# A softmax on one core: the first store enters the transfer queue when group 4 has been scaled

## The chip, the core and the metric

The kernel runs on one core of a Trainium2 chip. A core has engines that work side by side, each with its own list of instructions: VectorE (DVE), ScalarE (ACT) and GpSimd (POOL) compute, SyncE (SP) here only waits and issues transfers. TensorE (PE) has no work in this kernel. Data move between the large memory (HBM) and the core's own memory (SBUF, 128 partitions) by transfers (DMAs) that run on 16 transfer engines of the core. The metric is the device time of one execution in microseconds (us).

## What is computed

A softmax over the last axis of an input of 16 x 1024 x 512 numbers of 4 bytes, that is 16,384 rows of 512, 33.55 MB in and 33.55 MB out:

```
x_max = np.max(x, axis=-1, keepdims=True)
exp_x = np.exp(x - x_max)
return exp_x / np.sum(exp_x, axis=-1, keepdims=True)
```

## The kernel before

**Tiles.** The 16,384 rows are taken as 128 rows per partition: each of the 128 partitions has 128 rows, numbered 0 to 127. Eight such rows on all partitions make a group (`GROUP`, 128x4096 numbers); there are 16 groups. Transfers move blocks of 16 rows per partition (`BLOCKS`), so two groups, 4096 KB each. There are eight loads and eight stores. I number both 0 to 7: load 0 and store 0 are the block (0, 16), load 5 is (80, 96), and so on. Within a block, a partition's 16 rows lie together in HBM, so one packet is 32 KB.

**The buffer.** `held` has room for 96 rows per partition (`RING`, 12 groups). Six blocks fit. Loads 6 and 7 reuse the place of blocks 0 and 1, and so must wait until stores 0 and 1 have landed.

**What is done to a group.** DVE takes the negated maximum of each row (`rowmax`, line 164). ACT takes the exponential of each row in place, with that maximum as bias, and sums it (line 195, eight instructions for a group). DVE takes the reciprocal of the sums (line 170), and the group is multiplied by it (line 172): by POOL for groups 0 to 11, by DVE for groups 12 to 15. The order of DVE's work is written out by hand in `VECTOR` (M is a maximum, P a scaling on POOL, V one on DVE).

**The order of transfers.** All 16 transfers are issued by SP into one queue, in the order of `ORDER`: loads 0 to 5, stores 0 to 2, loads 6 and 7, stores 3 to 7. The first six loads wait for nothing (`AHEAD`), and the first of them is moved ahead of the program's opening barrier (`loads_at_the_head`). Behind them, the loop of lines 140 to 154 writes SP's list. For a load it puts a wait for the store that must have landed (`stored`) ahead of the issue. For a store it puts waits for the groups that the block holds: each group `g` has a semaphore `scaled[g]`, which the scaling of that group raises, and the set `done` sees to it that each is waited for once:

```
for g in range(GROUPS):
    if meets(k, *group(g)) and g not in done:
        take(nc.sync, scaled[g], 1)
        done.add(g)
```

So store 0 waits for groups 0 and 1, store 1 for groups 2 and 3, store 2 for groups 4 and 5. `take` (line 110) is a wait on the engine's own list: what stands behind it on that engine waits too. After the last issue SP waits for all stores to land, which ends the program.

Of the kernel before, what the change touches and what calls it, by code (L numbers as in the profile page):

```python
# [1 line left out]

# [4 lines left out]

F32 = mybir.dt.float32
EXP = mybir.ActivationFunctionType.Exp
AX = mybir.AxisListType.X  # L10

GROUP = 8
GROUPS = 16
RING = 12 * GROUP

BLOCKS = [(0, 16), (16, 32), (32, 48), (48, 64), (64, 80), (80, 96), (96, 112), (112, 128)]
ORDER = [
    ("L", (0, 16)),
    ("L", (16, 32)),
    ("L", (32, 48)),
    ("L", (48, 64)),
    ("L", (64, 80)),
    ("L", (80, 96)),
    ("S", (0, 16)),
    ("S", (16, 32)),  # L30
    ("S", (32, 48)),
    ("L", (96, 112)),
    ("L", (112, 128)),
    ("S", (48, 64)),
    ("S", (64, 80)),
    ("S", (80, 96)),
    ("S", (96, 112)),
    ("S", (112, 128)),
]
AHEAD = 6  # L40

VECTOR = """
    M0 M1 P0 M2 P1 M3 P2 M4 P3 M5 P4 M6 P5 M7 P6 M8 P7 M9 P8 M10 P9 M11
    P10 M12 P11 M13 V12 M14 V13 M15 V14 V15
"""

AT_HEAD = {mybir.EngineType.SP: 1}

def loads_at_the_head(nc):

    main, body = nc.main_func.blocks[0], nc.main_func.blocks[1]
    for engine, count in AT_HEAD.items():
        loads = [
            i
            for i in body.instructions
            if i.engine == engine and type(i).__name__ == "InstDMACopy"  # L60
        ][:count]
        barrier = next(
            n
            for n, i in enumerate(main.instructions)
            if i.engine == engine and type(i).__name__ == "InstDrain"
        )
        for load in loads:
            body.instructions.remove(load)
        main.instructions[barrier:barrier] = loads


@with_exitstack
def kernel(
    ctx: ExitStack,
    tc: tile.TileContext,
    x: bass.AP,
    out: bass.AP,
):
    nc = tc.nc
    nc.at_finalize(loads_at_the_head)  # L80
    P = nc.NUM_PARTITIONS

    d = x.shape[-1]
    x_rows, out_rows = x.flatten_outer_dims(), out.flatten_outer_dims()
    assert x_rows.shape[0] == GROUPS * GROUP * P

    def in_dram(rows, a, b):

        first, last = next(k for k in BLOCKS if k[0] <= a and b <= k[1])
        block = rows[first * P : last * P].rearrange("(p r) d -> p r d", p=P)  # L90
        return block[:, a - first : b - first, :]

    held = nc.alloc_sbuf_tensor("held", [P, RING, d], F32).ap()
    shift = nc.alloc_sbuf_tensor("shift", [P, GROUPS * GROUP], F32).ap()
    sums = nc.alloc_sbuf_tensor("sums", [P, GROUPS * GROUP], F32).ap()
    recip = nc.alloc_sbuf_tensor("recip", [P, GROUPS * GROUP], F32).ap()

    loads = [k for what, k in ORDER if what == "L"]
    stores = [k for what, k in ORDER if what == "S"]
    loaded = {k: nc.alloc_semaphore(f"loaded{k[0]}") for k in loads}  # L100
    scaled = [nc.alloc_semaphore(f"scaled{g}") for g in range(GROUPS)]
    stored = {k: nc.alloc_semaphore(f"stored{k[0]}") for k in stores}
    maxed = nc.alloc_semaphore("maxed")
    expd = nc.alloc_semaphore("expd")
    to_pool = nc.alloc_semaphore("to_pool")
    to_vector = nc.alloc_semaphore("to_vector")

    def take(engine, semaphore, n):

        engine.wait_ge(semaphore, n).then_inc(semaphore, -n)  # L110

    def rows(a, b):
        assert a // RING == (b - 1) // RING
        return held[:, a % RING : (b - 1) % RING + 1, :]

    def meets(k, a, b):
        return k[0] < b and a < k[1]

    def group(g):
        return g * GROUP, (g + 1) * GROUP  # L120

    def stats(t, g):
        return t[:, g * GROUP : (g + 1) * GROUP]

    def load(k):
        copy = nc.sync.dma_start(out=rows(*k), in_=in_dram(x_rows, *k))
        copy.then_inc(loaded[k], 16)
        return copy

    with tc.manual_schedule():
        for _, k in ORDER[:AHEAD]:
            tc.no_tile_sem_insts.add(load(k).ins.name)
    tc.close()
    tc.compile()  # L137

    taken, done = set(), set()
    for what, k in ORDER[AHEAD:]:  # L140
        if what == "L":
            for s in stores:
                if meets(s, k[0] - RING, k[1] - RING) and s not in taken:
                    take(nc.sync, stored[s], 16)
                    taken.add(s)
            load(k)
        else:
            for g in range(GROUPS):
                if meets(k, *group(g)) and g not in done:
                    take(nc.sync, scaled[g], 1)  # L150
                    done.add(g)
            nc.sync.dma_start(out=in_dram(out_rows, *k), in_=rows(*k)).then_inc(
                stored[k], 16
            )


    seen = set()

    def rowmax(g):
        for k in loads:  # L160
            if meets(k, *group(g)) and k not in seen:
                take(nc.vector, loaded[k], 16)
                seen.add(k)
        nc.vector.reduce_max(  # L164
            out=stats(shift, g), in_=rows(*group(g)), axis=AX, negate=True
        ).then_inc(maxed, 1)

    def scale(g, engine, ready):
        take(nc.vector, expd, 1)
        nc.vector.reciprocal(out=stats(recip, g), in_=stats(sums, g)).then_inc(ready, 1)  # L170
        take(engine, ready, 1)
        engine.tensor_mul(  # L172
            out=rows(*group(g)),
            in0=rows(*group(g)),
            in1=stats(recip, g).unsqueeze(2).to_broadcast([P, GROUP, d]),
        ).then_inc(scaled[g], 1)

    for step in VECTOR.split():
        what, g = step[0], int(step[1:])
        if what == "M":  # L180
            rowmax(g)
        elif what == "V":
            scale(g, nc.vector, to_vector)
        else:
            scale(g, nc.gpsimd, to_pool)


    nc.scalar.preload_act_table(EXP)  # L188

    with nc.scalar.Fori(0, GROUPS) as i:  # L190
        take(nc.scalar, maxed, 1)
        for r in range(GROUP):
            row = held[:, bass.ds(i % (RING // GROUP) * GROUP + r, 1), :]
            at = bass.ds(i * GROUP + r, 1)
            act = nc.scalar.activation(  # L195
                out=row,
                in_=row,
                func=EXP,
                bias=shift[:, at],
                scale=1.0,  # L200
                accum_out=sums[:, at],
            )
        act.then_inc(expd, 1)


    for k in stores:
        if k not in taken:
            take(nc.sync, stored[k], 16)


# [1 line left out]
_INS = ['x']  # L212
_OUTS = [((16, 1024, 512), 'float32')]


# [23 lines left out]
```

## Time and profile before

| | before |
|---|---|
| time, median of 3 runs | 160.15 us (160.12 to 160.21) |
| the profiled execution | 160.14 us, its span 158.8 us |
| busy: DVE, ACT, POOL | 90.6 (57%), 92.0 (58%), 84.0 us (53%) |
| one scaling on POOL (line 172) | 7015 ns, x12 |
| one scaling on DVE (line 172) | 4570 ns, x4 |
| one row maximum on DVE (line 164) | 4399 ns, x16 |
| one exponential on ACT (line 195) | 712 ns, x128 |
| loads, issue to landing | 12.2 / 29.7 / 58.8 us (shortest, median, longest) |
| stores, issue to landing | 17.9 / 28.3 / 38.3 us |

The span is the stretch from the first to the last instruction of the program; the rest of the execution's time lies around it. A time within the span is counted from its start. "Issue to landing" is the time from SP's issue of a transfer to the moment when its semaphore shows that all of it has arrived, so it holds the time that the transfer stands in the queue behind others. In the view by stretches, each line is a stretch of the span, its length, and what happened in it: the share in which the 16 transfer engines were busy, and the GB/s that they moved. A packet is counted whole in the stretch in which it starts, which is why the share of a short stretch can be over 1.

### The profile page before, as it was taken

The numbers are of one execution on the slowest core, as the hardware profiler recorded it, in microseconds if no ns is written. First come the engines' busy times: TensorE is split into PE (matmuls) and PEld (weight loads), VectorE is DVE, ScalarE is ACT, GpSimd is POOL, SyncE is SP. The second block draws the span as 40 slices with busy tenths as digits, with TensorE's granted clock in tenths as the row PEclk, the third lists the DMA queues.
The fourth block names the chain that finished last, engine by engine and source line by source line (L and its number), as shares of the span: only waits on it lengthen the run. The fifth ranks groups of instructions, "written<-read, shape, count | busy, mean of one in ns | idle before, by whom it ended". The sixth has DMA issues, their size and how long they took to land. (4 is left out here: it accounts for less than half of the span.)

```text
span 158.8 us, 747 instructions
## 1 busy us (share of the span) xinstructions
DVE 90.6 (57%) x36; ACT 92.0 (58%) x257; POOL 84.0 (53%) x16
## 2 busy tenths in 40 slices
DVE  0008959777977977887700000795999998640000
ACT  0300699999999999999993000059934929200000
POOL 0000009999999999999999999259200000000000
DMA  7999999999999998999999999999999999999996
GB/s 264 470 454 396 413 487 421 396 454 470 396 396 487 437 396 380 413 396 454 470 396 421 462 437 396 446 479 396 421 446 454 396 437 473 413 404 454 446 413 264
DMA packets 2305, 67.12 MB, mean 423 GB/s; under 512 B 256, under 2 KB 256, under 8 KB 256
## 3 DMA queue, kind: packets, MB, share of 16 engines
q1 hardware_dynamic: 2304, 67.11, 98.9%
q14 instruction: 1, 0.01, 0.0%
HBM read 33.55 MB, written 33.55 MB: 423 GB/s over the span
## 5 line engine op out<-in xcount | busy, mean ns | idle before, releaser
L195 ACT ACTIVATE held<-held,shift x128 | 90.3, 712 | 40.0 <-ACTq L110 40.0
L172 POOL TENSOR_TENSOR held<-held,recip 128x4096 f32<-128x4096 f32 x12 | 83.8, 7015 | 28.0 <-POOLq L110 28.0
L164 DVE TENSOR_REDUCE shift<-held 128x8 f32<-128x4096 f32 x16 | 70.3, 4399 | 33.2 <-DVEq L110 33.2
L195 ACT ACTIVATION_READ_ACCUMULATOR held<-held,shift x128 | 24.6, 192 | 0.0
L172 DVE TENSOR_TENSOR held<-held,recip 128x4096 f32<-128x4096 f32 x4 | 18.3, 4570 | 0.6
L170 DVE RECIPROCAL recip<-sums 128x8 f32<-128x8 f32 x16 | 3.2, 201 | 16.5 <-DVEq L110 16.5
L188 ACT ACT_TABLE_LOAD x1 | 1.3, 1283 | 3.9 <-PEq L137 3.9
L223 POOL MEMSET const-float32-0.0<- 128x1 f32 x1 | 0.1, 98 | 0.2 <-issue 0.2
L223 POOL MEMSET const-uint8-127<- 128x1 uint8 x1 | 0.1, 102 | 0.0
L223 POOL MEMSET const-bfloat16-1.0<- 128x1 bf16 x1 | 0.1, 101 | 0.0
L223 POOL MEMSET const-float32-1.0<- 128x1 f32 x1 | 0.1, 98 | 0.0
## 6 DMA issues: line engine op xcount, KB each, us to landing
held<-in_x_dram SPq DMA_DIRECT2D x8, 4096.0 KB, 29.7
out_dram<-held SPq DMA_DIRECT2D x8, 4096.0 KB, 28.3
```

The source lines that it names most:

```text
L164: nc.vector.reduce_max(out=stats(shift, g), in_=rows(*group(g)), axis=AX, negate=True).then_inc(maxed, 1)
L170: nc.vector.reciprocal(out=stats(recip, g), in_=stats(sums, g)).then_inc(ready, 1)
L172: engine.tensor_mul(out=rows(*group(g)), in0=rows(*group(g)), in1=stats(recip, g).unsqueeze(2).to_broadcast([P, GROUP, d]),).then_inc(scal ...
L188: nc.scalar.preload_act_table(EXP)
L195: act = nc.scalar.activation(out=row, in_=row, func=EXP, bias=shift[:, at], scale=1.0, accum_out=sums[:, at],)
L223: nc = _bacc.Bacc("TRN2", target_bir_lowering=False, num_devices=1)
```

## The change

A table `AFTER` names, for a block that is stored, one more group that must have been scaled before its store is issued. It has one entry: the store of block (0, 16) also waits for group 4. The loop that writes SP's waits looks the table up:

```diff
+AFTER = {(0, 16): 4}
...
             for g in range(GROUPS):
-                if meets(k, *group(g)) and g not in done:
+                if (meets(k, *group(g)) or AFTER.get(k) == g) and g not in done:
                     take(nc.sync, scaled[g], 1)
                     done.add(g)
```

With it store 0 waits for groups 0, 1 and 4, store 1 for groups 2 and 3, and store 2 for group 5 alone, since group 4 has been waited for by then. The order in which the transfers are issued is the same, and so are the lists of DVE, ACT and POOL.

## The prediction

> **What bounds the kernel now.** I read the queue table of the page first, because the share of the transfer engines decides whether anything else matters; then the timeline of SP and POOL, which dates the issue that is moved; then the landings of single transfers; then stretches of 1.21 us, cut to one packet per engine, to see where the stream loses time.
>
> From the page, the queue and the volume (queue, packets, MB, share of 16 engines):
>
> ```profile
> q1 hardware_dynamic: 2304, 67.11, 98.9%
> HBM read 33.55 MB, written 33.55 MB: 423 GB/s over the span
> ```
>
> One queue holds everything, 16 transfers of 4096 KB, and it is busy for 98.9% of the span. So the time is the length of this stream, and the change can only matter by a hole that it closes or opens in it. The stretches below show what a full stream is. Columns: stretch in us, its length, clock, share of the transfer engines, GB/s; a packet counts where it starts.
>
> ```profile
> 0.00:1.00 1.00, 1.00 0.00 0
> 1.00:1.50 0.50, 1.00 3.12 852
> 1.50:2.00 0.50, 1.00 0.53 197
> 2.00:2.75 0.75, 1.00 0.00 0
> 2.75:3.40 0.65, 1.00 1.90 807
> ...
> 54.88:56.09 1.21, 1.00 1.01 433
> 56.09:57.30 1.21, 1.00 1.01 433
> 57.30:58.51 1.21, 1.00 1.14 433
> 58.51:59.72 1.21, 1.00 1.59 433
> 59.72:60.93 1.21, 1.00 0.44 190
> 60.93:62.14 1.21, 1.00 1.01 433
> ...
> 59.72:60.60 0.88, 1.00 0.00 0
> 60.60:61.20 0.60, 1.00 2.04 874
> 61.20:61.80 0.60, 1.00 0.00 0
> 61.80:62.40 0.60, 1.00 2.02 874
> ...
> 107.82:109.03 1.21, 1.00 1.01 433
> 109.03:110.24 1.21, 1.00 1.01 433
> ```
>
> A stretch of 1.21 us with 433 GB/s is 524 KB: one packet of 32 KB on each of 16 engines, a round. A transfer is 8 rounds, about 9.7 us. One stretch breaks the rhythm: 59.72 to 60.93 us has 190 GB/s, so 1.21 x (1 - 190/433) = 0.68 us is missing, and the two stretches ahead of it already have a share of 1.14 and 1.59: their packets take longer. This is the place where load 5 (the sixth, rows 80 to 96) ends and store 0 begins. The landings agree. Load 4 is issued at 2.16 us and lands 48.9 later, at 51.1; load 5 is issued at 2.65 and lands here:
>
> ```profile
> L126 SPq DMA_DIRECT2D held<-in_x_dram x1: 487/487/487, 2.6 to 2.6; - x1
> DMA to landing us min/median/max: 58.8/58.8/58.8
> ```
>
> That is 61.4, so 10.4 us after load 4 in place of 9.7: 0.7 us lost. By the first packets it is a little more: store 0 starts at 60.6, and eight rounds of 1.21 after load 5's first packets (about 50.1) would be 59.8. I call it the pause, 0.7 to 0.87 us, 0.8 in the sum. The other change from loading to storing (load 7 to store 3, near 109.1) has two full stretches and no pause; nor has store 2 to load 6.
>
> Now the issues and what they wait for:
>
> ```profile
> 0.00 3.13 SPq L126 DMA_DIRECT2D held<-in_x_dram  x6
> 37.54 28.23 SPq L152 DMA_DIRECT2D out_dram<-held  x3
> ...
> 51.36 7.01 POOL L172 TENSOR_TENSOR held<-held,recip 128x4096 f32<-128x4096 f32 x1
> ```
>
> Store 0 goes out at 37.54, when the queue still holds more than 20 us of loads. Group 4 is the fifth scaling of POOL, 51.36 + 7.01 = 58.37 us.
>
> **The change, part by part.** No instruction of DVE, ACT or POOL is added, removed or moved. On SP the wait for group 4 moves from store 2 to store 0.
>
> - *The wait.* SP gets past it at 58.40 and issues store 0 at 58.40 + 0.07 = 58.47 (before, the same step took 37.47 to 37.54). That is 20.9 us later.
> - *What is queued behind it on SP.* Store 1 went out at 51.49 and now follows store 0, with two waits of 0.07 that are met and an issue of 0.35: about 58.96. Its data are due 9.7 us after store 0's, so this costs nothing. Store 2 still waits for group 5 (65.37) and goes out at 65.44 as before. Load 6 waits for store 0 to land (71.2) while two more stores, 19.4 us, are queued, so its delay by any fraction of a microsecond is covered. At the end the last store is issued at 140.91 and can start only when store 6 is through, which lands at 125.56 + 23.5 = 149.1: some 7 us of cover. POOL and DVE wait for none of these issues.
> - *Does the queue run dry?* Load 5's data, without the pause, end at 59.8 on the first engines and about 60.3 on the last (the rounds are spread over 0.5 us). What an issue into idle engines costs is shown once, by load 0: issued at 0.00, 13 of 16 first packets start between 1.0 and 1.5 us, three between 1.5 and 2.0, and the second round starts between 2.75 and 3.40. So a first round takes 1.7 to 1.9 us where a warm one takes 1.21. Put behind 58.47: store 0's first packets at 59.5 to 60.4, its second round at 61.2 to 61.9. Before, the second round started from 61.8 to 62.4. If load 0 is the right pattern and nothing is added, the stream is ahead by 0.5 to 0.6: I take 0.55.
> - *Bounds.* Below: the pause goes and the store is there in time, second round at 59.8 + 1.21 = 61.0: ahead by 0.8. Above: the cold first round of load 0 and the pause on top, 61.55 + 0.87 = 62.4 on average against 62.1, behind by 0.3; if these engines take as long to start again as load 0's slowest (up to 0.4 later than its average), behind by 0.5 or a little more.
> - *Sum.* The profiled execution took 160.14 us, its span 158.8, so 1.3 lie around the span; the median of the runs shown is 160.15. 160.14 - 0.55 = 159.6.
>
> The Trainium skill speaks against the change: "DMA: Bandwidth & Descriptors", section "Rules for kernel authors", says to issue a transfer early and wait for it late, so that its fixed setup cost lies beside other work. By that rule issuing 20.9 us later can only expose a cost; it is the rival with the dry queue below. In this trace store 0 was issued early, and the pause is there all the same. The same page, "Two DMAs through the same engine are not ordered", states that transfers on one queue start in order but are pipelined, with the reading and the writing side of an engine separate; that would let a queued store begin inside load 5's last packets, and the shares of 1.14 and 1.59 before the missing stretch agree with it.
>
> **The rivals.**
>
> - *The pause belongs to the first store wherever it comes* (the first transfer out of the buffer or into the output): for it, that no later change of direction has it. Then it is paid between 59.5 and 60.4 as it was between 58.5 and 60.6, and the time stays at 160.1. Against: load 0 was the first of everything too, and its first round cost only 0.5 to 0.7 beyond a warm one.
> - *The pause goes whole.* The store that lies queued for 20 us slows the last loads, and one that arrives with their end doesn't; the engines take it over warm. 160.14 - 0.8 = 159.3. Against: store 3 lies queued for 28 us (issued at 81.5, running from 109) and slows nothing.
> - *The queue runs dry* (slower). Group 4 is ready 1.4 us before load 5's data end, and load 0 shows 1.0 to 1.9 from issue to first packet. The engines go idle, start cold, and the first store's own pause comes after it, uncovered: 0.3 to 0.6 behind, 160.5 with a reach to 160.7. It decides from the point where store 0's second round starts later than 62.1 on average, 3.6 us after its issue in place of load 0's 3.1.
> - *It doesn't do what it says.* SP's order shows store 0 behind groups 0, 1 and 4, store 1 behind 2 and 3, store 2 behind 5. If group 4 were ready no later than now that is 58.4 in any case. I give it nothing of its own.
>
> **How the numbers follow.** What a measurement of this kernel can tell from no change is about 0.2%, 0.32 us: below 159.83 is faster, above 160.47 slower. Forecast (ahead by 0.35 to 0.7, 159.6): 0.34. Pause gone whole (159.3): 0.16. Same pause, same place (160.1): 0.18. Dry queue (160.5 to 160.7 and a little beyond): 0.32, high because the cover is shorter than the slowest start that load 0 shows. So faster 0.50, same 0.18, slower 0.32. The range reaches from the pause gone whole, 159.25, to the dry queue's 160.65; the forecast's own is 159.4 to 159.8.
>
> **What would show it.** Right: load 5 lands near 60.7 in place of 61.4; the stretches of 1.21 us up to 59.7 keep a share of 1.0; store 0, issued at 58.5, has its first packets between 59.5 and 60.4, some of them 1.7 to 2.1 us long, and lands near 70.6; every later landing is earlier by the same 0.5, and the last store's issue keeps its cover. Wrong: load 5 still lands at 61.4 (the pause isn't the queued store's doing); or no packet starts for more than 1.5 us around 60 (dry). A span shorter than 158.8 with all landings up to store 0 unchanged would mean that the gain is not from here.

## The result and the profile after

The changed kernel takes 160.64 us (median of 14 runs, 160.49 to 161.36) against 160.13 us for the kernel before (14 runs beside it): ratio 1.0037, 95% interval 1.0027 to 1.0048. It is slower by 0.5 us. I had forecast 159.6.

The profiled execution took 161.36 us with a span of 160.0, more than the median. A second trace of the same kernel, the first of the experiments below, has 160.54 and 159.2. Both lose time at the same places; in the first, one engine loses about 1 us more than the others.

The queue and the volume of the kernel after (queue, packets, MB, share of 16 engines):

```profile
q1 hardware_dynamic: 2304, 67.11, 98.5%
HBM read 33.55 MB, written 33.55 MB: 419 GB/s over the span
```

The same bytes in the same number of packets, 4 GB/s slower. SP's issues in the timeline of the kernel after (start, length, count):

```profile
0.00 3.18 SPq L129 DMA_DIRECT2D held<-in_x_dram  x6
58.45 7.30 SPq L155 DMA_DIRECT2D out_dram<-held  x3
70.51 10.14 SPq L129 DMA_DIRECT2D held<-in_x_dram  x2
80.84 60.43 SPq L155 DMA_DIRECT2D out_dram<-held  x5
```

Store 0 goes out at 58.45, as worked out. Now the stream of the kernel after in stretches of one round, at the three places where the direction changes: load 5 to store 0, store 2 to load 6, load 7 to store 3 (columns as in the prediction):

```profile
56.23:57.44 1.21, 1.00 1.01 433
57.44:58.65 1.21, 1.00 1.01 433
58.65:59.86 1.21, 1.00 1.01 433
59.86:61.07 1.21, 1.00 1.01 433
...
86.41:87.62 1.21, 1.00 1.00 433
87.62:88.83 1.21, 1.00 1.28 433
88.83:90.04 1.21, 1.00 0.96 406
...
105.01:106.22 1.21, 1.00 1.00 433
106.22:107.43 1.21, 1.00 1.38 433
107.43:108.64 1.21, 1.00 1.41 406
108.64:109.85 1.21, 1.00 0.44 190
109.85:111.06 1.21, 1.00 1.01 433
```

The pause at 60 us is gone without a trace: every stretch is full, and store 0 follows load 5 without a gap. But around 88 us packets grow longer (share 1.28), and at 106 to 110 us stands the pattern that was at 57 to 61 before: two stretches with a raised share (here 1.38 and 1.41), then one with 190 GB/s. In the kernel before, the same two places are full:

```profile
88.46:89.67 1.21, 1.00 0.94 406
89.67:90.88 1.21, 1.00 1.01 433
...
107.81:109.02 1.21, 1.00 1.01 433
109.02:110.23 1.21, 1.00 1.01 433
```

(The 406 is one packet that starts a little outside its stretch; the next is on time.)

To compare runs I use one number for each place. The 16 engines report the landing of a transfer one by one; I take the mean of the 16 times, subtract that of the transfer ahead, and subtract the 9.69 us that 16 rows take at full rate (fewer for a transfer that was cut). What is left is lost. Store 2 and load 6 are added up, since the change from storing to loading shifts a landing from the one to the other.

| kernel | store 0 issued | load 5 | store 2 + load 6 | load 7 | sum |
|---|---|---|---|---|---|
| before | 37.5 us | 0.76 | 0.02 | 0.03 | 0.81 |
| after, first trace | 58.5 us | 0.03 | 0.29 | 0.98 | 1.30 |
| after, second trace | 58.6 us | 0.03 | 0.32 | 0.85 | 1.20 |

The sum rises by 0.4 to 0.5, and the median by 0.51. So at its own place the change won 0.73 us, more than was forecast. It lost 0.3 and 0.8 to 0.95 us at two places 30 and 50 us later, which had been free.

### The profile page after: what moved, and what is told of

Same layout as the page of the kernel before. It is cut to its first block, busy times and chain, and to the rows that moved or that the text cites. A ratio compares the mean times of both kernels' runs of the same rounds, so it can differ in the third digit from the quotient of the medians.

```text
span 160.0 us, 747 instructions
## 1 busy us (share of the span) xinstructions
DVE 90.6 (57%) x36; ACT 92.0 (57%) x257; POOL 84.0 (52%) x16
```

## The experiments

**The two kernels again, and other groups for store 0.** The first question was whether the places are fixed, or chance.

> The changed kernel, unaltered, for a second trace. Theory 'moved toll' (a load that ends with a store already lying in the queue pays a pause once; store 0 issued late only passes it on to the next such place): load 5 lands near 60.7 us with full stretches, as in the first trace, and a loss of about 1 us stands again at the end of load 7 (106 to 110 us) and perhaps a third of a us at the end of store 2 (87 to 89.5). Theory 'chance' (other traffic on the chip stops the stream now and then): the losses stand elsewhere, or are missing. Theory 'dry queue': a hole in the stream around 60 us and none later. The single packet of 2.7 us on one engine in the first trace should not be back, so the span should be near 159.3.

> The kernel before, unaltered, for a second trace. Moved toll: the pause of 0.7 to 0.9 us stands again at the end of load 5 (58.5 to 60.6 us), and the ends of store 2 and load 7 are full; span 158.8. Chance: the pause stands elsewhere or is missing.

```diff
-AFTER = {(0, 16): 4}
+AFTER = {(0, 16): 3}
```

> Store 0 waits for group 3 in place of group 4, so it is issued near 51.5 us, 7 us before the place where load 5 slows down. Moved toll: this is queued early enough, the pause of 0.7 to 0.9 us is back at the end of load 5, the end of load 7 is full again, and the time is that of the kernel before, 160.1. If any lateness of store 0 costs by itself, the time lies between 160.1 and 160.6, with the loss at load 7.

The same line with a 5:

> Store 0 waits for group 5 and is issued near 65.4 us, when load 5 has long ended (60.3). This makes the queue dry on purpose and prices a cold start: a hole from 60.3 to about 66.5, so 6.0 to 6.7 us in all. Dry queue and moved toll agree on that; moved toll adds the loss of about 1 us at the end of load 7, so 160.15 - 0.8 + 6.3 + 1.0 = 166.6. If the pause is the first store's own price, it is paid at store 0's first round here and the end of load 7 is full: about 166.4, with first packets of 2 us or more.

| run | store 0 issued | load 5 | store 2 + load 6 | load 7 | time |
|---|---|---|---|---|---|
| after again | 58.6 | 0.03 | 0.32 | 0.85 | 160.76 (before 160.14) |
| before again | 37.7 | 0.63 | 0.03 | 0.16 | 160.14 |
| group 3 | 51.5 | 0.58 | 0.03 | 0.05 | 160.15, ratio 1.0002 (0.9993 to 1.0012) |
| group 5 | 65.4 | 0.02, then a hole of 6.27 | 0.92 | 0.86 | 167.54 |

Both kernels lose at the same places in both of their traces, so chance is out. With group 3, store 0 is 14 us later than before and nothing changes: lateness as such costs nothing. With group 5 the queue does run dry. The stretches of that kernel around the hole:

```profile
59.20:60.40 1.20, 1.00 0.01 0
60.40:66.20 5.80, 1.00 0.00 0
66.20:66.60 0.40, 1.00 3.09 1311
66.60:67.40 0.80, 1.00 0.00 0
67.40:67.80 0.40, 1.00 3.17 1311
```

Store 0 is issued at 65.42; all its first packets start between 66.2 and 66.6, and the second round 1.2 us later. So a store into idle engines needs about 0.9 us from issue to first packet, and its first round is as short as any other. That refutes "the first store's own price", and it shows why the changed kernel's queue didn't run dry: 58.45 + 0.9 is ahead of load 5's end, 59.9 on the first engine and 60.06 on average. The Trainium skill, "DMA: Bandwidth & Descriptors", section "Specifications", gives a first-byte latency of about 0.6 us for transfers issued from SP. This trace agrees, if one counts from the end of the 0.35 us issue instruction: 0.5 to 0.6.

What the expectation didn't have: store 2's end pays 0.92 here. 167.54 is 0.9 above the forecast of 166.6, and that is this loss. In the changed kernel, whose queue didn't run out wholly, the same place paid 0.3.

**Taking the queued successor away.** In the next runs transfers are cut in two, and the transfer that changes the direction waits until the first part has landed. The edit, besides the cuts in `ORDER` (here store 2 and load 7 into 12 and 4 rows):

```diff
+HOLD = {('L', (96, 112)): ('S', (32, 44)), ('S', (48, 64)): ('L', (112, 124))}
...
     for what, k in ORDER[AHEAD:]:
+        if (what, k) in HOLD:
+            first, part = HOLD[what, k]
+            if first == "L":
+                nc.sync.wait_ge(loaded[part], 16).then_inc(passed[part], 1)
+            else:
+                take(nc.sync, stored[part], 16)
+                taken.add(part)
```

DVE then waits on `passed` for that part. Not shown: at the end of its list SP also waits for each such part of a load. The span ends 0.03 us behind the last landing without such a part, 0.10 behind it with one and 0.17 with two, and the times of these runs hold that too. With the cuts alone and `HOLD` empty:

> Control for the next two: the changed kernel with store 2 cut into 12 and 4 rows and load 7 into 12 and 4 rows, nothing waiting for the parts. If cutting costs nothing by itself: the time of the changed kernel, 160.6 to 160.8, with losses of about 0.35 us at the end of store 2 and 0.9 us at the end of load 7 as in its two traces.

With both entries:

> The same, but each transfer that changes the direction is issued only when 12 of the 16 rows of the transfer ahead of it have landed, so about 1.9 us before that one's data end: load 6 behind store 2, store 3 behind load 7 (and store 0 behind group 4 as in the changed kernel). Theory 'queued change' (a pause is paid only where the transfer of the other direction lies in the queue well before the one ahead ends): no pause anywhere, span near 157.9, time 159.3, faster than both. Theory 'toll' (the loss is owed at some change of direction and only moves): it shows up at another place, time 160.1 to 160.7. Theory 'dry queue': holes at the two new places, 160.6 and more.

With store 3's entry alone, and store 2 whole:

> The changed kernel with store 3 alone issued when 12 rows of load 7 have landed; load 6 still lies queued behind store 2. Queued change: the pause at the end of load 7 is gone, the one at the end of store 2 stays at 0.35 us: 160.65 - 0.9 = 159.75. Toll: what load 7 no longer pays is paid at store 2 or later, 160.1 to 160.7.

| run | load 5 | store 2 + load 6 | load 7 | time, ratio to before |
|---|---|---|---|---|
| cuts alone | 0.03 | 0.55 | 0.82 | 161.03, 1.0058 (1.0034 to 1.0083) |
| load 6 and store 3 late | 0.03 | 0.74 | 0.10 | 160.31, 0.9999 (0.9987 to 1.0012) |
| store 3 late | 0.03 | 0.37 | 0.11 | 160.06, 0.9993 (0.9981 to 1.0004) |

What was left in the queue when a transfer was issued I count from its issue to the mean end, over the 16 engines, of the last packets ahead of it, taken at full rate. By that the late issues came 1.3 to 1.7 us ahead, not the 1.9 of the expectations, and the changed kernel's store 0 came 1.6 us ahead (60.06 - 58.45).

Store 3, issued 1.7 us ahead of load 7's end, frees that end: 0.85 to 0.98 becomes 0.1, and 160.64 becomes 160.06. That kernel's views of load 6, of the second part of load 7 and of store 3 (issue instruction in ns, start; then us from issue to landing):

```profile
L134 SPq DMA_DIRECT2D held<-in_x_dram x1: 340/340/340, 70.6 to 70.6; - x1
DMA to landing us min/median/max: 29.3/29.3/29.3
...
L134 SPq DMA_DIRECT2D held<-in_x_dram x1: 1238/1238/1238, 80.7 to 80.7; - x1
DMA to landing us min/median/max: 29.0/29.0/29.0
...
L167 SPq DMA_DIRECT2D out_dram<-held x1: 343/343/343, 107.4 to 107.4; - x1
DMA to landing us min/median/max: 11.9/11.9/11.9
```

Load 6 lands at 70.6 + 29.3 = 99.9 and load 7 at 80.7 + 29.0 = 109.7: 9.8 apart, so next to nothing is lost. (In the first trace of the changed kernel load 7 landed at 111.5, 11.2 behind load 6.) Store 3 lands at 107.4 + 11.9 = 119.3, one full transfer later, so its late issue costs nothing either. The time is above the 159.75 that "queued change" gave: the mean landing of the last store is 0.31 us earlier than in the kernel before, but the last engine's only 0.18, and the wait more at the end takes 0.07 of that.

Load 6 is another matter. Issued about as late (1.3 us) it is worse off than queued: 0.74 against 0.55 in the run with the cuts alone, and 0.37 with store 2 whole. Its first packets start on time but take up to 2.2 us, as load 0's do, where a store's into idle engines took 1.24 (3.09 x 0.40 us, in the stretches of group 5). Why a load starts slower, no run here shows. So "queued change" fits the stores and not the load, and 159.3 was not reached. Cutting store 2 seems to cost 0.2 by itself (0.55 against 0.32).

**Emptying the queue where no direction changes.** The kernel before, with store 0 early; store 1 cut into 12 and 4 rows, and store 2 held for the 12:

> The kernel before, with store 1 cut into 12 and 4 rows and store 2 issued only when the 12 have landed. Here the queue nearly empties between two stores, where no direction changes, and store 0 lies early in the queue as before. Theory 'emptied queue' (once the queue has all but run out, the later changes of direction pay): the pause of 0.8 us stays at load 5, and the ends of store 2 and load 7 lose 0.35 and 0.9 us as in the changed kernel: 161.4. Theory 'first change pays' (the first change of direction with a queued successor pays, the later ones don't): only load 5 pays, 160.1.

The same cut, nothing held:

> Control for the run in which store 2 was held back until 12 rows of store 1 had landed: the kernel before with store 1 cut into 12 and 4 rows and nothing waiting for them. Emptied queue: the cut alone changes nothing, the pause stays at load 5, store 2 and load 7 end free, 160.15. If the cut was what brought the later losses: 161.4 again.

Issues of the kernel with store 2 held (the four stores from 37.70 include store 2, at 78.65), and its stretches at the ends of load 5 and load 7:

```profile
37.70 41.28 SPq L167 DMA_DIRECT2D out_dram<-held  x4
79.09 2.20 SPq L134 DMA_DIRECT2D held<-in_x_dram  x2
81.48 60.01 SPq L167 DMA_DIRECT2D out_dram<-held  x5
```

```profile
57.32:58.53 1.21, 1.00 1.09 433
58.53:59.74 1.21, 1.00 1.54 433
59.74:60.95 1.21, 1.00 0.76 325
...
106.42:107.63 1.21, 1.00 1.35 433
107.63:108.84 1.21, 1.00 0.97 298
108.84:110.05 1.21, 1.00 0.43 135
```

| run | load 5 | store 2 + load 6 | load 7 | time, ratio to before |
|---|---|---|---|---|
| store 2 held | 0.61 | 0.26 | 0.89 | 161.37, 1.0079 (1.0055 to 1.0102) |
| cut alone | 0.74 | 0.00 | 0.05 | 160.27, 1.0008 (0.9997 to 1.0018) |

This is the run that decides. Store 0 is queued early, load 5 pays as before, no direction changes where the queue nearly empties (1.6 us were left when store 2 came), and still the two later places pay, with the numbers of the changed kernel: 0.26 and 0.89. The time is the 161.4 that the emptied queue gave, not the 160.1 of "first change pays"; all four runs (161.27 to 161.80) lie above all ten of the control (160.07 to 160.68), which excludes the cut. Load 6 also goes out later than before, at 79.1 in place of 71.3, but some 11 us ahead of its turn, and in the kernel with group 3 a store issued 9 us ahead cost no more than one issued 23 us ahead. Store 3's issue is where it was, at 81.5, and it is load 7's end, ahead of it, that loses most.

**How much must be left in the queue?** Load 5 cut into 8 and 8, and into 10 and 6 rows, with store 0 held for the first part in place of group 4:

> The kernel before with load 5 cut into 8 and 8 rows; store 0 waits for the landing of the first 8 instead of group 4 and is issued near 56 us, 4 us before load 5's data end. Theory 'emptied queue' (what makes the later changes of direction pay is that the queue all but ran out, not the lateness as such): 4 us are left in the queue, so the pause of 0.6 to 0.8 us is paid at load 5 and the end of load 7 is free, 160.15. Theory 'lateness' (each us by which store 0 comes later shifts some of the loss): part of the pause at load 5 and part of the 0.9 us at load 7, 160.3 to 160.5.

> As the run with load 5 cut into 8 and 8 rows, but cut into 10 and 6, so that store 0 is issued near 57.5 us, 2.7 us before load 5's data end; that run (issue at 56.3) paid 0.43 us at load 5 in place of 0.6 to 0.76, and nothing at load 7. Theory 'emptied queue': if 2.7 us are enough to keep the queue from running out, less than 0.43 is paid at load 5 and nothing later, 159.8; if not, load 5 ends free and load 7 pays 0.9, as in the changed kernel, 160.65. Theory 'lateness': some of both, the sum no smaller than in the kernel before, 160.2 to 160.5.

And load 6 a little earlier, behind 10 rows of store 2, with the other two late:

> As the run with all three changes of direction issued late, but load 6 goes out when 10 of store 2's 16 rows have landed in place of 12, so about 3.1 us before store 2's data end in place of 1.9. There the late load left a hole of 0.67 us and no pause, while the two late stores cost nothing. If 1.2 us more hides the load's start and is still too late for a pause: nothing lost at any of the three, 160.15 - 0.75 = 159.4, faster than both kernels. If load 6 now pays the pause of a queued load (0.3 to 0.4 us): 159.75, as with store 3 alone issued late. If the hole stays: 160.1.

| run | left in the queue | load 5 | store 2 + load 6 | load 7 | time |
|---|---|---|---|---|---|
| store 0 at 56.3 | 3.8 us | 0.48 | 0.02 | 0.06 | 160.21 (before 160.15) |
| store 0 at 57.4 | 2.8 us | 0.11 | 0.12 | 0.33 | 160.35 (before 160.24) |
| load 6 at 86.5 | 2.6 us | 0.03 | 0.42 | 0.10 | 160.27 (before 160.15) |

(The 0.48 holds 0.05 for the cut; the expectations name the rest, 0.43.) It is graded, which neither theory had in that form. With 3.8 us left the later places stay free, as "emptied queue" had it, and load 5 pays a little less; with 2.8 us load 5 is all but free, and load 7 pays a third. The time, 160.35, is where "lateness" put it, but not for its reason: the sum falls to 0.56 in place of staying. The time doesn't follow the sum, because the end of the span is the end of the slowest engine, and at load 7 the engines fare very differently: by their packets, five of the 16 lose 0.1 us or less, and six 0.5 or more, one of them 1.0. So the third is a mean over engines that pay and engines that don't. Load 6 at 2.6 us pays 0.42, as when queued, and the time, 160.27, is above the 159.75 that went with that.

**Store 3's issue.** In the traces where load 7 pays 0.8 us or more, the issue instruction of store 3, right behind load 7's, is longer: 1.1 us in the changed kernel, 0.69 in the kernel before. Was the pause made there? The changed kernel with store 3 also waiting for group 8, or 10, and the kernel before with group 8 for store 3:

```diff
-AFTER = {(0, 16): 4}
+AFTER = {(0, 16): 4, (48, 64): 8}
```

> The changed kernel, and store 3 also waits for group 8, so it is issued near 86.3 us, some 23 us before load 7's data end and 6 us after load 7's own issue. In every trace where load 7's end pays 0.8 us or more, store 3's issue instruction, 0.5 us behind load 7's, took 1.06 to 1.12 us in place of 0.33; where that end is free or nearly so it took 0.63 to 0.91. Theory 'emptied queue': the loss comes from the state that the late store 0 leaves, store 3 is still queued early, so load 7 pays 0.9 and store 2 0.3: 160.65. Theory 'stalled issue' (the pause at load 7 is made when store 3 is put in right behind load 7): store 3's issue takes 0.33 us, load 7 ends free, and with load 5 free as well 160.65 - 0.9 = 159.75.

> The changed kernel, and store 3 also waits for group 10: issued near 100.3 us, 9 us before load 7's data end. Emptied queue: still queued early, load 7 pays 0.9, 160.65. Stalled issue: free, 159.75. If the distance from the end alone counts, as with store 0 (at 9 us it paid 0.58, at 4 us 0.43): about 0.6 at load 7, 160.3.

> Control on the kernel before: store 0 early, store 3 held until group 8, near 86.3 us. Emptied queue: nothing changes, 0.7 at load 5 and nothing at load 7, 160.15. Stalled issue: the same, since the end of load 7 is nearly free already; at most 0.1 is won.

| run | store 3 issued | its issue | load 5 | store 2 + load 6 | load 7 | time, ratio to before |
|---|---|---|---|---|---|---|
| after, group 8 | 86.3 | 0.34 us | 0.03 | 0.26 | 0.90 | 160.68, 1.0031 (1.0021 to 1.0040) |
| after, group 10 | 100.3 | 0.34 us | 0.03 | 0.33 | 0.88 | 160.66, 1.0023 (1.0014 to 1.0032) |
| before, group 8 | 86.2 | 0.34 us | 0.62 | 0.04 | 0.03 | 160.21, 1.0002 (0.9993 to 1.0011) |

Load 7's end in the first of these:

```profile
107.41:108.62 1.21, 1.00 1.42 406
108.62:109.83 1.21, 1.00 0.70 298
```

The issue is short and the pause is there, so a stall at the issue is not its cause; the long instruction is a sign that goes along with it. And whether store 3 comes 28, 23 or 9 us ahead of load 7's end makes no difference.

**The two best together.** Store 0 at 57.5 (load 5 in 10 and 6), and store 3 behind 12 rows of load 7:

> The two changes that lost least, together: store 0 issued near 57.4 us (load 5 cut into 10 and 6 rows, as in the run that paid 0.11 there, 0.12 around store 2 and 0.33 at load 7, but nearly 1 us on one engine), and store 3 issued when 12 of load 7's 16 rows have landed, which left load 7 free with store 0 at 58.5. Theory 'emptied queue': the state that a late issue leaves shows only at a change of direction with a queued successor, and load 7 no longer has one, so the sum of the losses is 0.11 + 0.12 + 0.1 = 0.33 in place of 0.81 in the kernel before: 160.2 - 0.5 = 159.7, faster than both. Theory 'toll': the loss turns up again, 160.1 to 160.4.

159.96 us against 160.14, ratio 0.9987 (0.9978 to 0.9996), with losses of 0.10, 0.13 and 0.10. The sum is the 0.33 that was worked out; the time is not the 159.7. The mean landing of the last store is at 157.75 us against 158.18 before, 0.43 earlier, but the last engine's at 158.51 against 158.78. That engine waits at 126 us for a packet of another queue, and store 4's landing is 0.49 later on it alone. (The kernel before has such a wait too, at 132 us.) The span ends a further 0.17 behind, with two waits more at its end. So this version is faster than the kernel before by a tenth of a per cent, where the changed kernel is slower by 0.4.

## Why the prediction was wrong

- *What bounds the kernel, the pause and its size.* Right: one stream, and the time follows its holes. The pause at load 5 was 0.76 by the mean of the landings, where I had taken 0.8.
- *The issue at 58.47 and what is queued behind it.* Right to 0.02 us. Store 1 followed at 58.98. Load 6, load 7 and the last stores kept their cover.
- *"Does the queue run dry?"* The term was mis-sized. I took load 0's first round, 1.7 to 1.9 us, for store 0's. A store's first round is as short as any (group 5: 1.2 us), and its packets start about 0.9 us after the issue. So store 0 was in time, and the gain at its place was the whole 0.73 and not 0.55. My rival "the pause goes whole" described this place rightly: load 5 landed at 60.7 and store 0 at 70.4. By itself this would have made the kernel faster.
- *The step that failed* is the term that the sum doesn't have: the two later changes of direction, put at nothing, so that "every later landing is earlier by the same 0.5". I had read from the trace of before that store 2 to load 6 and load 7 to store 3 are free, and took that for a property of those places. It isn't: issuing store 0 1.6 us ahead of load 5's end lets the queue run down, and then these two pay 0.3 and 0.9 us, 1.2 against the 0.73 won. The held store 2 shows that the emptying is enough, without a late store 0 and without sparing load 5 its pause.
- *The rivals.* "The pause belongs to the first store" fell: store 0 pays nothing at 58.5 or 65.4. The dry queue named 160.5 to 160.7, and 160.64 came. That is luck, for its mechanism is not what happened: no stretch around 60 us is short of packets. Most of the loss is 50 us away from where it put it.
- *The rule of the Trainium skill* ("DMA: Bandwidth & Descriptors", "Rules for kernel authors": issue early) gave the right side. This trace shows no fixed cost exposed at the late transfer, though; what was lost, was lost at later ones. For a load the rule holds at its own place: load 6, issued 1.3 us ahead, opened 0.7 us.

What stays open is what the emptied queue changes. The traces show that the last round ahead of a change of direction, at the end of a load often the last two, grows long on most engines, where a transfer of the other direction lies queued and the queue had been down to about 1.6 us some time before (on some engines, at 2.8 us). The start of the program may count as such a state, and then load 5's pause in the kernel before is the same thing; no run tried that apart. What in the transfer engines or the queue keeps that state is not shown either.

## What to carry to other kernels

Where one queue is the bound, a transfer that is issued late changes more than its own start: look at every later change of direction for a loss that moved there, and add up the whole stream before judging one place. A free handover in a trace is no promise that it stays free after an edit ahead of it. In this kernel a store could be issued 1.3 to 1.7 us ahead of its turn at no cost at its own place, a load (1.3 us) couldn't; and a gain in the mean over the transfer engines counts only as far as the slowest engine has it.

## What the runs showed of the hardware that I had not expected

- A store into idle engines starts its packets 0.9 us after its issue, with a first round of 1.2 us; the first round of a load into idle engines (load 0) takes 1.2 to 2.5 us, 1.8 to 2.0 on average.
- After a queue that was down to about 1.6 us, later changes of direction cost 0.3 us (storing to loading; 0.9 where it had run dry) and 0.9 us (loading to storing), if the next transfer lay queued; with 3.8 us left they stayed free.
- One packet of 8 KB of the instruction queue, 0.31 us long, at 125 to 139 us of every trace, holds up one of the 16 engines by 0.3 to 0.7 us; in the last run above that engine is the one that ends last.
